# Block 1 of a two-block decoder layer: the first norm's scale moves from the input to the results of the products

## The chip, the cores and the metric

The kernel runs on one core of a Trainium2 chip. A time is the device time of one execution in microseconds (us); a kernel's time is the median over its runs. In the trace PE is the matrix engine, PEld its loading of the stationary operand, DVE the vector engine, ACT the scalar engine, POOL the general-purpose engine and SP the engine whose queue issues most DMA transfers. Times inside a profile count from the start of its span.

## The reference, cut to what matters

A token has 1024 values, there are 256 tokens, and everything is fp32. The first block begins like this:

```python
def rmsnorm(x, g):
    xf = x.astype(jnp.float32)
    y = xf * lax.rsqrt(jnp.mean(xf * xf, axis=-1, keepdims=True) + EPS) * g.astype(jnp.float32)
    return y.astype(x.dtype)

h = rmsnorm(x, attn_pre_norm[l])
proj = h @ w_in[l]
a_cols, f_cols, m_cols = jnp.split(proj, [SWA_COLS, SWA_COLS + FOX_COLS], axis=-1)
```

`a_cols` holds queries, keys and values of a sliding-window attention (512, 128 and 128 columns), `f_cols` queries, keys, values and four gate logits of a forgetting attention (256, 256, 256, 4), `m_cols` the latents of a third attention (416 columns), whose parts get norms of their own. Three attentions, an output product, a convolution feed-forward, and a second block (gated linear attention, pooling, a mixture of 32 experts) follow; none of them is touched. The mean of squares is one number per token, so the norm's scale can be multiplied onto the row of `proj` as well as onto the row of `x`.

## The kernel before, in words

Tokens are two tiles of 128 (t = 0, 1). `x` lies with tokens on partitions; a product needs the contracted dimension there, so `x` is transposed on PE, 128x128 at a time, against an identity matrix loaded from memory (`c_ident`). To keep fp32 accuracy every operand of a large product is split into a high part (a rounded copy, ACT, line 228 for weights and 445 for `hT`) and a low part (the rest, DVE, lines 229 and 446), and a product is three matmuls for each 128 contracted rows: high by high, high by low, low by high (line 131 holds every matmul).

`first_norm(t)` (lines 433 to 447) takes the sum of squares of tile t, forms the reciprocal root (five short DVE steps and one ACT step, line 406), multiplies the scale onto both halves of the tile (`xs`, line 439), transposes eight 128x128 pieces into two PSUM banks, and evacuates each piece twice, as `hH` (ACT, with the norm's gain `g_col` as a column per partition) and as `hL` (DVE). `g_col` comes by a transfer that gathers 1024 single values into columns (line 478).

All weights pass through a ring of four 1 MB buffers `raw`. `add_load` lists the loads in order, `pump(n)` issues the next n, and `drop` hands a buffer back and issues one more. The order here is `vf` (388 columns: both value groups and the gate logits, in two loads by rows, each in two column pieces), `sk` (keys), `sq` 0 and 1 (queries), `ml` 0 and 1 (latents), `fq`, `fk`, then the output product's weights. The x tiles are issued ahead of them on SP.

A unit is a piece of a product: `prep` splits its weights, `run` multiplies and evacuates. `feed` runs a list of units with the `prep` of three further ones ahead. `units_a` (`vf`, `ml`) has tokens on the result's partitions: two PSUM banks, one for each tile; for `vf` the matmuls of tile 1 are held until the last `vf` weights and then run in one go. `unit_b` (`sk`, `sq`, `fq`, `fk`) has columns on partitions and both tiles beside each other, 8 x 3 matmuls of 256 columns. Results are evacuated by `vf_evac` (656, 657), `k_evac` (650, which writes each key group to both partition halves), and `act.mul` or `act.copy` for queries and `fk` (661, 925, 926).

Behind the first query unit stands `bias_rows` (606): a small matmul, a DVE addition (609), a store to memory (`dsc`), two loads that read it back in a skewed form (POOL's queue), and two DVE copies (616) into `bias`, which the sliding-window scores need. The constant `tri` of the gate sums (782) is issued on POOL's queue behind these.

The order of each engine's instructions is set ahead of time by the framework's planner: it walks the program with a model of durations and lets each engine take what is ready in the model, earlier program order first. On the chip an engine then keeps that order, whatever comes late. `issue_after(i)` puts the block's instructions behind instruction i.

Of the kernel before, what the change touches and what calls it, by code (L numbers as in the profile page):

```python
# [9 lines left out]
F32 = mybir.dt.float32  # L10
# [90 lines left out]
def emit(ctx, tc, I, C, out, dump=None, stop=None):  # L101
# [272 lines left out]
    last_pow, last_sq, last_v = [None], [None], [None]  # L374
# [15 lines left out]
    def rstd_halves(h0, h1, dve_half, by_sqrt=False):  # L390
# [14 lines left out]
        if by_sqrt:  # L405
            act.activation(out=r[:, 1:2], in_=v[:, 0:1], func=ACTF.Sqrt)
            dve.reciprocal(r[:, 2:3], r[:, 1:2])
            dve.scalar_tensor_tensor(out=r[:, 3:4], in0=r[:, 2:3], scalar=r[:, 2:3], in1=v[:, 0:1],
                                     op0=ALU.mult, op1=ALU.mult)
            dve.tensor_scalar(out=r[:, 4:5], in0=r[:, 3:4], scalar1=-0.5, scalar2=1.5, op0=ALU.mult, op1=ALU.add)  # L410
            dve.tensor_tensor(out=r[:, 0:1], in0=r[:, 4:5], in1=r[:, 2:3], op=ALU.mult)
            return r
# [20 lines left out]
    def first_norm(t):  # L433

        h0, h1 = x[:, t, 0:512], x[:, t, 512:1024]
        r = rstd_halves(h0, h1, t == 0, True)
        for q in range(2):
            xs = yp.tile([128, 512], F32, name="xs", tag="xs", bufs=2)
            dve.tensor_scalar(out=xs, in0=x[:, t, q * 512:(q + 1) * 512], scalar1=r[:, 0:1], scalar2=None, op0=ALU.mult)
            b = bank()  # L440
            for i in range(4):
                last_mm[0] = pe.transpose(b[:, tk(i)], xs[:, tk(i)], ident)
            for i in range(4):
                k = 4 * q + i
                act.mul(hT[0][:, k, tk(t)], b[:, tk(i)], g_col[:, k:k + 1])
                dve.scalar_tensor_tensor(out=hT[1][:, k, tk(t)], in0=b[:, tk(i)], scalar=g_col[:, k:k + 1],
                                         in1=hT[0][:, k, tk(t)].bitcast(F32), op0=ALU.mult, op1=ALU.subtract)
# [31 lines left out]
    ident = cload("ident", [128, 128], eng=act)  # L479
# [17 lines left out]
    for i in range(2):  # L497
        cols_load(("vf", i), w1, 4 * i, 4, 640, 128, 388, [(128, 1280, 260)])
# [71 lines left out]
    pump(NA)  # L570
# [3 lines left out]
    keep_warm(0, ones)  # L574
    for t in range(2):
        first_norm(t)
        keep_warm(0 if t else 4)
    dump("hH", hT[0].bitcast(F32))
    dump("hL", hT[1].bitcast(F32))
    if stop == "hT":  # L580
        return
# [64 lines left out]

    def k_evac(ps):
# [7 lines left out]
    def vf_evac(t, ps):  # L655
        dve.tensor_tensor(out=fz[:, t, :], in0=ps[:, 384:388], in1=fbB, op=ALU.add)
        act.copy(vf[:, t, :], ps[:, 0:384])
# [3 lines left out]
             + [cols_unit("sq", c // 2, c % 2, lambda ps, c=c: act.mul(qT[:, c, :], ps, 0.125)) for c in range(4)])  # L661
    feed(units[:6] + [then(bias_rows)] + units[6:])
# [252 lines left out]
    def mla_v(kt, h):  # L915
# [5 lines left out]
    feed(units_a("ml", 416, hT, lambda t, ps: ml_ps.__setitem__(t, ps)), rr(swa_all, gate_steps), 2)  # L921
# [3 lines left out]
    feed([cols_unit("fq", 0, c, lambda ps, c=c: act.mul(fqT[:, c, :], ps, 0.125)) for c in range(2)]  # L925
         + [cols_unit("fk", 0, c, lambda ps, c=c: act.copy(fkT[:, c, :], ps)) for c in range(2)], side, 3)
# [911 lines left out]
```

## Time and profile before

| | us |
|---|---|
| median of 3 runs (lowest, highest) | 720.93 (720.68, 722.7) |
| the profiled execution: its own time | 718.01 |
| the profiled execution: its span | 716.2 |
| PE busy in the span | 655.2 (91%) |
| DVE busy | 377.4 (53%) |
| ACT busy | 307.1 (43%) |

The profiled execution is 1.8 us longer than its span, which runs from the first to the last instruction. A busy PE is not a PE at its peak, since matmuls overlap; where PE is dense, one 128x256 matmul starts 0.12 us after the one before it. The chain of waits that ended last lies on PE's matmuls for 59% of the span, and for 20% on the transfers of the expert weights, which fill the stretch from 513 to 653 us.

### The profile page before, as it was taken

How to read it: one execution, taken by the hardware profiler on the slowest of the kernel's cores; microseconds unless marked ns; L12 is line 12 of the kernel's file. 1: busy time of each engine (PE TensorE's matmuls, PEld its weight loads, DVE VectorE, ACT ScalarE, POOL GpSimd, SP SyncE). 2: the span in 40 equal slices, each digit the busy share in tenths (PEclk: the TensorE clock that was granted, in tenths of full speed). 3: DMA queues.
4: the chain of work that ended last, by engine and by line, in shares of the span. 5: the costliest groups of instructions: out<-in, count | busy, mean ns of one | idle time of the engine just before them, and what ended most of it. 6: DMA issues, size and time to landing. Idle time of an engine off the chain costs nothing.

```text
span 716.2 us, 12560 instructions
## 1 busy us (share of the span) xinstructions
PE 655.2 (91%) x5084; PEld 536.4 (75%) x5084; DVE 377.4 (53%) x735; ACT 307.1 (43%) x580; POOL 43.1 (6%) x76
## 2 busy tenths in 40 slices
PE   5999899999999999999999999998999897786992
PEld 4988787999999999978988999987454543442650
DVE  6666577797778777673552755948232211120112
ACT  6739545475657555552932455535220101020111
POOL 5010020100000000002140000000000000000000
PEclk9999999999999999999999999999999999898996
DMA  9973309536556855661392499668999999999971
GB/s 279 322 240 124 112 1 343 174 132 240 197 184 193 278 177 177 220 192 34 89 240 59 153 357 391 232 228 317 381 416 422 423 422 423 423 421 424 422 257 63
DMA packets 82560, 182.31 MB, mean 255 GB/s; under 512 B 10689, under 2 KB 58049, under 8 KB 72256
## 3 DMA queue, kind: packets, MB, share of 16 engines
q1 hardware_dynamic: 78544, 175.27, 67.3%
q0 software_dynamic: 2624, 5.84, 2.6%
q8 instruction: 42, 0.69, 0.4%
q10 hardware_dynamic: 1328, 0.33, 0.2%
q14 instruction: 22, 0.18, 0.1%
HBM read 180.40 MB, written 1.06 MB: 253 GB/s over the span
## 4 chain that ended last, share of the span: by engine, by line
PE 62%; DMA 23%; DVE 6%; issue 4%; ACT 3%; POOL 1%; POOLq 0%; DVEq 0%; SPq 0%; ACTq 0%
PE bank L131 59%; DMA raw<-in_w_exp_up_dram 7%; DMA raw<-in_w_exp_gate_dram 7%; DMA raw<-in_w_exp_down_dram 6%; DMA S<-in_const_tri_dram 1%; DVE wL L229 1%; DMA S<-in_const_oh_rel_dram 1%; ACT S L681 1%; PE bank L689 1%; DMA dsc<-S 1%; DMA S<-in_pool_scale_dram 1%; DVE S L730 1%; PE bank L430 0%; DVE x L458 0%; DVE bank L454 0%
## 5 line engine op out<-in xcount | busy, mean ns | idle before, releaser
L229 DVE TENSOR_TENSOR wL<-raw,wH 128x1024 fp32r<-128x1024 f32 (+3 forms) x120 | 140.6, 1175 | 70.9 <-ACT wH L228 70.5
L228 ACT ACTIVATE wH<-raw 128x1024 fp32r<-128x1024 f32 (+3 forms) x120 | 121.7, 1022 | 109.7 <-PE bank L131 95.0
L131 PE MATMUL bank<-hH,wH 128*128 128x256 f32 (+1 forms) x496 | 141.8, 286 | 0.2 <-ACT wH L228 0.2
L131 PE MATMUL bank<-hL,wH 128*128 128x256 f32 (+1 forms) x496 | 140.2, 283 | 0.0
L131 PE MATMUL bank<-hH,wL 128*128 128x256 f32 (+1 forms) x496 | 140.1, 283 | 0.0
L131 PEld LDWEIGHTS bank<-hH,wH 128*128 128x128 f32 (+1 forms) x496 | 94.3, 190 | 3.2 <-ACT wH L228 1.2
L131 PEld LDWEIGHTS bank<-hL,wH 128*128 128x128 f32 (+1 forms) x496 | 94.3, 190 | 0.8
L131 PEld LDWEIGHTS bank<-hH,wL 128*128 128x128 f32 (+1 forms) x496 | 94.3, 190 | 0.3
L131 PE MATMUL bank<-raw,xg 128*32 128x256 f32 x1024 | 75.8, 413 | 13.9 <-DMA raw<-in_w_exp_up_dram 12.1
L131 PEld LDWEIGHTS bank<-raw,xg 128*32 128x32 f32 x1024 | 36.9, 118 | 45.0 <-DMA raw<-in_w_exp_up_dram 15.6
L1711 ACT ACTIVATE a<-bank,wsl 128x256 f32<-128x256 f32 x8 | 3.8, 474 | 108.8 <-PE bank L131 108.8
L1458 DVE SCALAR_TENSOR_TENSOR a<-bank,wsl,a 128x256 f32<-128x256 f32 x8 | 3.9, 483 | 82.2 <-ACT a L1711 82.2
L986 DVE SCALAR_TENSOR_TENSOR u<-bank,convp,u 128x255 f32<-128x255 f32 (+1 forms) x88 | 41.6, 479 | 6.9 <-ACT u L983 5.7
L131 PE MATMUL bank<-wH,hH 128*128 128x512 f32 (+3 forms) x108 | 39.9, 370 | 0.3 <-ACT hH L237 0.3
L131 PE MATMUL bank<-wH,hL 128*128 128x512 f32 (+3 forms) x108 | 39.1, 362 | 0.2 <-DVE hL L238 0.2
L131 PE MATMUL bank<-wL,hH 128*128 128x512 f32 (+3 forms) x108 | 38.7, 360 | 0.6 <-DVE wL L229 0.6
L131 PE MATMUL bank<-hH,wHL 128*128 128x256 f32 x192 | 36.6, 283 | 0.0
L1747 ACT ACTIVATE y<-bank,wsl 128x256 fp32r<-128x256 f32 (+1 forms) x24 | 13.1, 545 | 52.3 <-PE bank L131 52.2
L1458 DVE SCALAR_TENSOR_TENSOR y<-bank,wsl,y 128x256 fp32r<-128x256 f32 (+1 forms) x24 | 13.2, 570 | 39.4 <-ACT y L1747 39.3
L131 PEld LDWEIGHTS bank<-hH,wHL 128*128 128x128 f32 x192 | 30.8, 192 | 0.2
L983 ACT ACTIVATE u<-bank,convp 128x256 f32<-128x256 f32 x44 | 24.1, 554 | 12.9 <-PE bank L131 10.4
L229 DVE TENSOR_TENSOR wHL<-raw,wHL 128x1024 fp32r<-128x1024 f32 (+2 forms) x23 | 27.5, 1201 | 3.8 <-ACT wHL L228 3.8
(387 smaller groups left out, 1178.5 us busy)
## 6 DMA issues: line engine op xcount, KB each, us to landing
raw<-in_w_exp_gate_dram SPq DMA_DIRECT2D x28, 1024.0 KB, 19.7
raw<-in_w_exp_up_dram SPq DMA_DIRECT2D x28, 1024.0 KB, 19.8
raw<-in_w_exp_down_dram SPq DMA_DIRECT2D x24, 1024.0 KB, 19.7
raw<-in_w_up_dram SPq DMA_DIRECT2D x22, 1024.0 KB, 6.3
raw<-in_w_in_dram SPq DMA_DIRECT2D x20, 1024.0 KB, 5.9
raw<-in_w_down_dram SPq DMA_DIRECT2D x11, 1024.0 KB, 6.8
raw<-in_w_out_dram SPq DMA_DIRECT2D x8, 1024.0 KB, 5.7
raw<-in_w_exp_down_dram SPq DMA_DIRECT2D x12, 512.0 KB, 8.7
```

The lines of the kernel that those rows point to most:

```text
L131: last_mm[0] = pe.matmul(o, lhsT=l, rhs=r, start=start, stop=stop_, **kw)
L228: act.activation(out=hv, in_=raw, func=ACTF.Copy)
L229: dve.tensor_tensor(out=lv, in0=raw, in1=hv.bitcast(F32), op=ALU.subtract)
L681: act.activation(out=S[:, i, :nk], in_=S[:, i, :nk], func=ACTF.Exp, bias=nm[:, i:i + 1], accum_out=l[:, i:i + 1])
L689: pe.transpose(b[:, tk(i)], P[:, i, tk(kt)], ident)
L730: dve.tensor_tensor_reduce(out=Ss[h // 4][:, h % 4, 0:nk], in0=bv[par][:, i, :], in1=bias[:, h, 256 - nk:256], op0=ALU.add, op1=ALU.max, s ...
L983: act.activation(out=u[:, i, :], in_=ps, func=ACTF.Identity, scale=convp[:, 2, jj:jj + 1], bias=convp[:, 3, jj:jj + 1])
L986: dve.scalar_tensor_tensor(out=u[:, i, d:], in0=ps[:, 0:256 - d], scalar=convp[:, 2 - d, jj:jj + 1], in1=u[:, i, d:], op0=ALU.mult, op1=AL ...
L1458: return dve.scalar_tensor_tensor(out=o, in0=a, scalar=sc, in1=b, op0=op0, op1=op1)
L1711: act.activation(out=a, in_=gu[:, 0:256], func=ACTF.Silu, scale=rsl)
L1747: act.mul(y[:, 0, 0:n], db, wsl)
```

## The change

Four things change, all in block 1.

The first loads: x tile 0, then the first `vf` load (now in four pieces, two rows of blocks at a time), then x tile 1, then the other weights. The identity goes first on ACT's queue; the gain comes as eight rows of 128 values and is turned into columns by one transpose on PE and a DVE copy.

`x_in(t)` transposes x unscaled, straight from the loaded tile, and evacuates it with the gain as before. Only then come the squares and the root of tile t, which end in `r1[:, t]`. `x_in(0)` stands ahead of the products, `x_in(1)` behind the second `vf` unit.

The scale goes on the results. Where tokens lie on partitions it is a column: `vf_evac` multiplies by `r1[:, t]` in the same two instructions, and `ml_evac` adds one ACT instruction that scales the bank in place. Where tokens lie along the free dimension, `scale_rows` builds a tile with the scales of all 256 tokens in every partition (a DVE multiplication of the identity, a matmul with ones, a DVE copy), and keys, queries, `fq` and `fk` are evacuated by DVE with `scaled`.

Six small matmuls on the identity (`keep_warm`) stand behind `x_in(0)`; before, there were four, behind tile 0.

```diff
+    def raw_to_hT(t, gain, hT, q):
+        b = bank()
+        for i in range(4):
+            last_mm[0] = pe.transpose(b[:, tk(i)], x[:, t, 512 * q + 128 * i:512 * q + 128 * i + 128], ident)
+        for i in range(4):
+            k = 4 * q + i
+            last_hH[0] = act.mul(hT[0][:, k, tk(t)], b[:, tk(i)], gain(k))
+            last_low[0] = dve.scalar_tensor_tensor(out=hT[1][:, k, tk(t)], in0=b[:, tk(i)], scalar=gain(k),
+                                                   in1=hT[0][:, k, tk(t)].bitcast(F32), op0=ALU.mult,
+                                                   op1=ALU.subtract)
+
+    def scale_rows(o, r, dg):
+        diag_rows(dg, r, 2)
+        b = bank()
+        mm(b[:, 0:256], ones, dg.rearrange("p t s -> p (t s)"), True, True)
+        dve.tensor_copy(out=o, in_=b[:, 0:256])
...
     dma(x[:, 0, :], I["x"][0, tk(0), :])
-    dma(x[:, 1, :], I["x"][0, tk(1), :])
-    g_col = const.tile([128, 8], F32, name="g_col")
-    dma(g_col, I["attn_pre_norm"].rearrange("o (k p) -> p (o k)", p=128), act)
     ident = cload("ident", [128, 128], eng=act)
+    g_row = yp.tile([128, 512], F32, name="xs", tag="xs", bufs=2)[0:8, 0:128]
+    dma(g_row, I["attn_pre_norm"].rearrange("o (k p) -> (o k) p", p=128), act)
+    g_col = const.tile([128, 8], F32, name="g_col")
+    r1 = const.tile([128, 2], F32, name="r1")
...
-    pump(NA)
+    pump(1)
+    dma(x[:, 1, :], I["x"][0, tk(1), :])
+    pump(NA - 1)
...
-    for t in range(2):
-        first_norm(t)
-        keep_warm(0 if t else 4)
+    b = bank()
+    pe.transpose(b[:, 0:8], g_row, ident[0:8, 0:8])
+    dve.tensor_copy(out=g_col, in_=b[:, 0:8])
+
+    def x_in(t):
+        for q in range(2):
+            raw_to_hT(t, lambda k: g_col[:, k:k + 1], hT, q)
+        with tc.issue_after(last_hH[0].ins), tc.issue_after(last_low[0].ins):
+            rstd_halves(x[:, t, 0:512], x[:, t, 512:1024], True, True, out=r1[:, t:t + 1])
+
+    x_in(0)
+    keep_warm(6)
...
+    def second_x():
+        with tc.issue_after(last_mm[0].ins):
+            x_in(1)
...
+    def scaled(o, ps, c_=1.0, p=slice(0, 128)):
+        dve.scalar_tensor_tensor(out=o, in0=ps, scalar=c_, in1=rB1[0][p], op0=ALU.mult, op1=ALU.mult)
+
     def k_evac(ps):
+        scale_rows(rB1[0], r1, rB1[1])
         for g in range(2):
             for r in range(2):
-                (act.copy if r else dve.tensor_copy)(kT[64 * r:64 * r + 64, g, :], ps[64 * g:64 * g + 64, :])
+                p = slice(64 * g, 64 * g + 64)
+                scaled(kT[64 * r:64 * r + 64, g, :], ps[p, :], p=p)
...
-             + [cols_unit("sq", c // 2, c % 2, lambda ps, c=c: act.mul(qT[:, c, :], ps, 0.125)) for c in range(4)])
-    feed(units[:6] + [then(bias_rows)] + units[6:])
+             + [cols_unit("sq", c // 2, c % 2, lambda ps, c=c: scaled(qT[:, c, :], ps, 0.125)) for c in range(4)])
+    feed(units[:2] + [then(second_x)] + units[2:6] + [then(bias_rows)] + units[6:])
...
+    def ml_evac(t, ps):
+        act.mul(ps, ps, r1[:, t:t + 1])
+        ml_ps[t] = ps
...
-    feed([cols_unit("fq", 0, c, lambda ps, c=c: act.mul(fqT[:, c, :], ps, 0.125)) for c in range(2)]
-         + [cols_unit("fk", 0, c, lambda ps, c=c: act.copy(fkT[:, c, :], ps)) for c in range(2)], side, 3)
+    feed([cols_unit("fq", 0, c, lambda ps, c=c: scaled(fqT[:, c, :], ps, 0.125)) for c in range(2)]
+         + [cols_unit("fk", 0, c, lambda ps, c=c: scaled(fkT[:, c, :], ps)) for c in range(2)], side, 3)
```

## Rows read from the trace of the kernel before

**Rows 1.** Waits of PE, 0 to 60 us: who for whom, us in total, times, longest.

```profile
PE bank L442 <- DVE xs L439: 7.6, 1, 7.6
PE bank L131 <- ACT trr L794: 0.6, 1, 0.6
```

**Rows 2.** Stretches: length, then busy us of PE, PEld, DVE, ACT, POOL; clock, DMA share, GB/s.

```profile
10.00:15.00 5.00, 4.42 (x28) 3.98 (x28) 4.61 (x13) 4.82 (x13) 2.28 (x5) 1.00 1.15 325
15.00:20.00 5.00, 4.76 (x26) 4.14 (x25) 4.62 (x12) 3.22 (x8) 0.00 (x0) 1.00 1.05 366
70.00:75.00 5.00, 5.00 (x33) 3.53 (x31) 4.96 (x14) 1.09 (x3) 0.00 (x0) 1.00 0.84 271
```

**Rows 3.** Timeline of PE: start, us, engine, line, operation, names, shape, count.

```profile
11.69 0.42 PE L131 MATMUL bank<-wH,hH 128*128 128x388 f32 x1
...
22.14 0.28 PE L131 MATMUL bank<-hH,wL 128*128 128x256 f32 x1
...
24.77 0.28 PE L131 MATMUL bank<-hH,wH 128*128 128x256 f32 x1
...
27.74 0.81 PE L131 MATMUL bank<-S 32*8 32x384 f32 x2
...
40.05 1.13 PE L131 MATMUL bank<-kT,qT 64*128 64x256 f32 x8
...
43.59 1.16 PE L131 MATMUL bank<-kT,qT 64*128 64x128 f32 x16
```

**Rows 4.** Timeline of ACT; in brackets the idle time before and what ended it.

```profile
1.24 0.60 ACTq L134 DMA_DIRECT2D c_ident<-in_const_ident_dram  x1
...
4.58 0.63 ACT L395 ACTIVATE junk<-x 128x512 bf16<-128x512 f32 x1 [1.43 <-DMA x<-in_x_dram]
...
7.11 0.63 ACT L395 ACTIVATE junk<-x 128x512 bf16<-128x512 f32 x1 [1.27 <-DMA x<-in_x_dram]
...
10.19 0.85 ACT L228 ACTIVATE wH<-raw 128x776 fp32r<-128x776 f32 x1 [0.86 <-DMA raw<-in_w_in_dram]
...
20.64 2.01 ACT L228 ACTIVATE wH<-raw 128x1024 fp32r<-128x1024 f32 x2 [2.00 <-DMA raw<-in_w_in_dram]
```

**Rows 5.** DMA issues: queue, operation, count, KB each, us from issue to landing.

```profile
c_ident<-in_const_ident_dram ACTq DMA_DIRECT2D x1, 64.0 KB, 6.2
...
g_col<-in_attn_pre_norm_dram ACTq DMA_DIRECT2D x1, 4.0 KB, 5.0
```

**Rows 6.** Groups of instructions, 0 to 50 us: busy us, mean ns, idle before.

```profile
L446 DVE SCALAR_TENSOR_TENSOR hL<-bank,g_col,hH 128x128 fp32r<-128x128 f32 x16 | 4.8, 342 | 0.7 <-ACT hH L445 0.7
...
L439 DVE TENSOR_SCALAR xs<-x,rsr 128x512 f32<-128x512 f32 x4 | 1.8, 484 | 0.1
...
L661 ACT ACTIVATE qT<-bank 128x256 f32<-128x256 f32 x4 | 1.5, 375 | 0.7 <-PE bank L131 0.7
...
L397 DVE CUSTOM_DVE_ANT_0 yg<-x 128x512 f32<-128x512 f32 x1 | 0.7, 692 | 3.5 <-DMA x<-in_x_dram 3.5
```

**Rows 7.** Timeline of DVE, 21 to 45 us.

```profile
21.73 1.23 DVE L229 TENSOR_TENSOR wL<-raw,wH 128x1024 fp32r<-128x1024 f32 x1 [1.23 <-ACT wH L228]
...
25.88 0.41 DVE L650 COPY kT<-bank 64x256 f32<-64x256 f32 x1
...
28.20 1.23 DVE L229 TENSOR_TENSOR wL<-raw,wH 128x1024 fp32r<-128x1024 f32 x1 [0.66 <-ACT wH L228]
29.46 0.55 DVE L609 TENSOR_TENSOR S<-bank,S 8x384 f32<-8x384 f32 x1
...
41.18 0.69 DVE L616 COPY bias<-S 128x1024 f32<-128x1024 f32 x1 [7.18 <-DMA S<-dsc]
...
43.96 0.69 DVE L616 COPY bias<-S 128x1024 f32<-128x1024 f32 x1 [1.15 <-DMA S<-dsc]
```

**Rows 8.** The chain that ended last, 30 to 46 us: start, us, what.

```profile
30.30 5.04 DMA dsc<-S
...
37.16 7.53 DMA S<-in_const_tri_dram
```

More of the change, by code (lines that the diff above doesn't have):

```diff
@@ L388, in diag_rows, with rstd_halves @@
                           in1=r[:, 0:n, None].to_broadcast([128, n, 128]), op=ALU.mult)
-    def rstd_halves(h0, h1, dve_half, by_sqrt=False):
+    def rstd_halves(h0, h1, dve_half, by_sqrt=False, out=None):
         s = sm.tile([128, 2], F32, name="ssq", tag="ssq")
@@ L410, in rstd_halves @@
             dve.tensor_scalar(out=r[:, 4:5], in0=r[:, 3:4], scalar1=-0.5, scalar2=1.5, op0=ALU.mult, op1=ALU.add)
-            dve.tensor_tensor(out=r[:, 0:1], in0=r[:, 4:5], in1=r[:, 2:3], op=ALU.mult)
+            dve.tensor_tensor(out=r[:, 0:1] if out is None else out, in0=r[:, 4:5], in1=r[:, 2:3], op=ALU.mult)
             return r
@@ L431, in norm_to_hT @@
             split_act([h[:, 4 * q:4 * q + 4, tk(t)] for h in hT], v3(b, 4, 128))
[L433 to L447, printed above, removed]
+    def raw_to_hT(t, gain, hT, q):
[13 more added lines that the diff above has]
+        dve.tensor_copy(out=o, in_=b[:, 0:256])
     def post(y, t, g):
@@ L497, in emit @@
     for i in range(2):
-        cols_load(("vf", i), w1, 4 * i, 4, 640, 128, 388, [(128, 1280, 260)])
+        add_load(("vf", i), [(lambda t, k=k, d0=d0, nn=nn: v3(t, 4, 388)[:, k:k + 2, d0:d0 + nn],
+                              w1[:, 4 * i + k:4 * i + k + 2, cc:cc + nn])
+                             for k in (0, 2) for d0, cc, nn in ((0, 640, 128), (128, 1280, 260))])
     cols_load(("sk", 0), w1, 0, 8, 512, 128)
@@ L645, in emit @@
     vf, fz = at("vf", [128, 2, 384]), at("fz", [128, 2, 4])
+    rB1 = []
+    def second_x():
+        with tc.issue_after(last_mm[0].ins):
+            x_in(1)
+        yg = yp.tile([128, 1024], F32, name="yg", tag="yg")
+        rB1.append(yg[:, 0:256])
+        rB1.append(v3(yg, 2, 128, 256))
+    def scaled(o, ps, c_=1.0, p=slice(0, 128)):
+        dve.scalar_tensor_tensor(out=o, in0=ps, scalar=c_, in1=rB1[0][p], op0=ALU.mult, op1=ALU.mult)
     def k_evac(ps):
+        scale_rows(rB1[0], r1, rB1[1])
         for g in range(2):
             for r in range(2):
-                (act.copy if r else dve.tensor_copy)(kT[64 * r:64 * r + 64, g, :], ps[64 * g:64 * g + 64, :])
+                p = slice(64 * g, 64 * g + 64)
+                scaled(kT[64 * r:64 * r + 64, g, :], ps[p, :], p=p)
     def cols_unit(key, i, c, evac):
@@ L655, in vf_evac @@
     def vf_evac(t, ps):
-        dve.tensor_tensor(out=fz[:, t, :], in0=ps[:, 384:388], in1=fbB, op=ALU.add)
-        act.copy(vf[:, t, :], ps[:, 0:384])
+        r = r1[:, t:t + 1]
+        dve.scalar_tensor_tensor(out=fz[:, t, :], in0=ps[:, 384:388], scalar=r, in1=fbB, op0=ALU.mult, op1=ALU.add)
+        act.mul(vf[:, t, :], ps[:, 0:384], r)
     units = (units_a("vf", 388, hT, vf_evac, True)
              + [unit_b(("sk", 0), lambda r: v3(r, 8, 128), 8, 128, hT, k_evac, True)]
-             + [cols_unit("sq", c // 2, c % 2, lambda ps, c=c: act.mul(qT[:, c, :], ps, 0.125)) for c in range(4)])
-    feed(units[:6] + [then(bias_rows)] + units[6:])
+             + [cols_unit("sq", c // 2, c % 2, lambda ps, c=c: scaled(qT[:, c, :], ps, 0.125)) for c in range(4)])
+    feed(units[:2] + [then(second_x)] + units[2:6] + [then(bias_rows)] + units[6:])
     b = bank()
```

11 lines of the change are left out of this document (3 added, 8 removed).

## The prediction

> **What bounds the kernel now.** I read the waits of PE first. In the first 60 us PE waits once for long, 7.6 us at the start, for the scaled halves of x (`xs`), and once for 0.6 us, for the `tri` constant [rows 1]. So block 1 has one gap worth the name, and behind it stands what feeds PE. The table of stretches comes next: from 10 to 20 us ACT and DVE are busy 8.0 and 9.2 of 10 us, while PE already counts as busy with matmuls that start one by one [rows 2]. In that stretch the reader should see that PE is paced by the splitting of weights and x, and that PE becomes dense only when the held `vf` matmuls of tile 1 are running. The timeline of ACT shows the third supplier: x tile 0 lands at 4.6, tile 1 at 7.1, the first `vf` weights at 10.2, the first query weights (`sq` 0) at 20.6, each time with ACT waiting [rows 4]. The share of the DMA engines is 1.05 to 1.15 there [rows 2], so these landings follow from the bytes ahead in the queue. Last comes the chain: from 30.3 to 44.7 us it runs through the store of the bias rows and the load of `tri` [rows 8], while PE works through queries and latents and ends up 0.6 us too early [rows 1]. From about 28 to 45 us both are equally long, so a gain counts only if the bias addition (line 609) moves as well as PE.
>
> **The start.** Removed ahead of the first transpose are the squares, the root and four `xs` of 0.48 us [rows 6]. The identity lands at 1.24 + 6.2 = 7.4 us [rows 4, 5], behind the gain, whose 4 KB take 5.0 us [rows 5]; without the norm it alone would hold PE until then. It goes first now, with eight rows instead of 1024 values behind it. Its landing is bounded by x tile 0, eight times as large, at 4.6 [rows 4], and by its old 6.2 us from half a microsecond earlier, 6.9; I take 4.6, nearest to a row without the single values. Weights lose x tile 1 in front of them: from tile 1 to `vf` 0 took 10.2 - 7.1 = 3.1 us [rows 4], so `vf` 0 is whole at 4.6 + 3.1 = 7.7 and its first half at about 6.1; with a high part of 0.85 us [rows 4] the first product starts near 7.2 instead of 11.69 [rows 3]. By the late identity the transposes come 2.3 us later, about 1.0 of it spare while the weights land and are split: 8.5. The lead here is 3 to 4.5 us.
>
> **Four loads become eight.** From tile 1 on, two `vf` transfers landed within 3.1 us [rows 4], the same rate as the 2.5 us of tile 1 alone for its smaller size, so I price the division at nothing; the cover is a queue that holds work until 20 us. The Trainium skill, DMA: Bandwidth & Descriptors, section Anatomy of one DMA, gives every transfer a fixed cost of some 2.0 us and its rules ask for 1 MB or more at a time. By that, four more transfers would cost 8 us if they stood one behind the other; two transfers in 3.1 us say that they overlap.
>
> **To the end of `vf` and `sk`.** DVE loses the four `xs` (1.8 us), gains one sum of squares (0.69 us [rows 6]), and does the eight low parts of tile 0 (8 x 0.34 = 2.7 us [rows 6]) before the weights land, where it used to be idle. The last `vf` matmul ended at about 22.1 [rows 3]. It cannot come earlier than the first product's lead allows (17.6), nor, if only DVE's 1.1 us and half of the 2.7 count, later than 19.7; I take 18.3. The 24 `sk` matmuls at 0.12 us follow (2 were done ahead, the other 22 last from 22.14 to 24.77 [rows 3]): 21.2.
>
> **The first query unit is where the lead shrinks.** Its weights landed at 20.6 with all the bytes ahead of them unchanged [rows 4]. Only the single values of the gain are gone; x tile 0 lands maybe 0.5 us earlier for it, so 20.1 to 20.6. High part 1.0 [rows 4], low part 1.23 [rows 7]: before, the low part was done at 22.96, with PE at the third matmul of the unit, which needs it, at 24.77 + 0.24 = 25.0 [rows 3, 7]. There are 2.05 us of slack, 2.55 with the earlier landing. So of about 4 us, 2.05 to 2.6 remain; I take 2.6, since 1024 separate values are the one thing in that queue unlike all others.
>
> **The bias addition.** Its matmul starts at 27.74 [rows 3], now 25.1. On DVE come new ahead of it: two more key evacuations at 0.41 [rows 7], a scale tile of 256 columns and its copy (bounded by 0.34 for 128 columns [rows 6] and 0.69 for 1024 [rows 7]; 0.4 each), one query evacuation (0.41, which took ACT 0.375 [rows 6]): together 2.0 us. DVE was idle for 1.23 and 0.66 us there, waiting for ACT's high parts [rows 7], which covers 1.9. So the addition moves from 29.46 [rows 7] to about 26.9; without that cover, to 28.5. The matmul with ones costs PE between 0.28 (a split 128x256) and 0.8 us (two of 384 columns) [rows 3]; none of it stays, as PE would otherwise wait from 21.2 for the query weights. The transfers behind the addition take 14.4 us as before [rows 8].
>
> **Later parts.** The two in-place scalings of `ml` cost ACT 0.4 to 0.6 us each by its 256-column row of 0.375 [rows 6]; I take nothing for them, because the latents wait for DVE's scores, and 0.5 as the bound. `fq` and `fk` add four evacuations to DVE, two of them near 66 to 75 us, where DVE is busy 4.96 of 5 us [rows 2]: 0 to 0.8, I take 0.3, since the other two fall where DVE has room. From there on every queue, buffer and transfer is released by computation, so the lead is handed on whole.
>
> **Sum.** 2.6 - 0 - 0.3 = 2.3 us. The profiled execution took 718.01 for a span of 716.2; it would take 715.7. The median of the runs is 2.9 above that execution, so I put the same 2.3 us on the median: 720.93 - 2.3 = 718.6. The forecast's own range is a gain of 1.6 to 3.0, or 717.9 to 719.3.
>
> **Rivals.**
> DVE eats the lead. The four key evacuations (4 x 0.41 = 1.7 us) become ready at 21 us, just when the first query's low part does; if they stand ahead of it, the unit starts 1.7 later and 0.9 remains: 720.0. For it: DVE takes ready work in program order, and the key unit precedes. Against: the query's weights are prepared three units ahead, so they precede in the program.
>
> The query weights land earlier. The gain rows of the output norm (line 670) are issued behind the last root, which now comes later; they and their successor are 128 copies of 4 KB each, 1 MB in all, and at 366 GB/s [rows 2] take 3 us of the same DMA engines. If they fall behind the query weights, the lead of `sk` is kept: 24.77 - 21.2 = 3.6, to 4.3 with `vf` at its early bound, less 0.3 for DVE: about 4, or 716.9. Against: nothing but that hint holds POOL back.
>
> Slower: query evacuations caught behind the bias copies. Queries leave PSUM on DVE now, and DVE stands still for 7.18 us until the read-back lands at 41.2, and again until 44.0 [rows 7]. PE needs queries 0 and 1 at 40.05 [rows 3]. If the planner, which models the transfers as faster, sets both copies ahead of query 1, that evacuation ends at 43.96 + 0.69 + 0.41 = 45.1, PE stands 5 us, 0.6 of which the wait for `tri` gives back: 4.4 lost against 2.6 gained, 722.7. It decides from query 1: if only queries 2 and 3 are caught, the scores at 43.59 [rows 3] wait until 45.5, 1.3 us net of the 0.6, and it is still faster. Against: query 1's product, the next after the bias matmul, is finished by 28.5 + 2.9 = 31.4, 10 us before the copies could run.
>
> Transfers don't overlap. Should each of the four extra ones hold the queue 0.9 us, a third of the pair's 3.1 us [rows 4], the query weights land 3.6 us later, at 23.7; the unit starts 1 us late instead of 2.6 early: 721.9. The skill's fixed cost per transfer, named above, would speak for it, and the trace against it.
>
> **How the numbers follow.** Forecast 0.47, DVE eats the lead 0.25, earlier weights 0.15, caught queries 0.11, serial transfers 0.02. A difference under 0.3%, 2.2 us, is what a measurement of this kernel can't tell from none, and the forecast lies just beyond it: I count 0.38 of its 0.47 as faster and 0.09 as same. Faster is 0.38 + 0.15 = 0.53, same 0.09 + 0.24 + 0.02 = 0.35, slower 0.11 + 0.01 = 0.12. The range reaches from 716.4, past the earlier weights, to 721.9 and leaves out the caught queries.
>
> **What would show it.** Right, if the first transpose starts near 4.6 and the first product near 7.2, PE is dense from about 14, ACT's wait for the first query weights grows and PE waits for their low part at about 22, and the bias addition and the landing of `tri` are both 2 to 3 us earlier. A first product later than 9, an addition later than 28.5, or a PE wait for `qT` near 38 to 45 us would show the step that is wrong. A lead that is there at 45 us and gone at the end would make the whole forecast wrong.

## The result, and the profile after

| | before | after |
|---|---|---|
| median, us (lowest to highest) | 720.55 (717.09 to 722.7), 20 runs | 726.75 (721.95 to 731.44), 20 runs |
| the profiled execution: own time, span | 718.01, 716.2 | 724.18, 722.4 |
| PE, DVE, ACT busy in it | 655.2, 377.4, 307.1 | 659.1, 381.5, 304.9 |

The ratio is 1.009, 95% interval [1.0073, 1.0107]: the change costs 6.2 us, where 2.3 us of gain had been forecast, and the time lies outside the range. One of the twelve runs of e15 below counts as slow; without it the median there is 723.91 us.

**Where it goes.** ACT loads a new function table at fixed places of the program, which makes milestones. These are the ones at the feed-forward and at the second block's products, and the last one ahead of the experts, before and after:

```profile
143.38 1.28 ACT L990 ACT_TABLE_LOAD   x1
355.38 1.28 ACT L1172 ACT_TABLE_LOAD   x1
495.10 1.28 ACT L141 ACT_TABLE_LOAD   x1
```

```profile
148.82 1.28 ACT L1025 ACT_TABLE_LOAD   x1
361.06 1.28 ACT L1207 ACT_TABLE_LOAD   x1
500.32 1.28 ACT L141 ACT_TABLE_LOAD   x1
```

Of the 6.2 us between the two spans, 5.4 are there at the first milestone. Up to the second 0.2 come in, up to the third 0.5 go, and the rest, 1.0, comes behind it. So there are two places to look: the first block, and a small loss near the end.

**The first block.** The waits of PE from 0 to 60 us, which answer to [rows 1]:

```profile
PE bank L584 <- DMA xs<-in_attn_pre_norm_dram: 5.5, 1, 5.5
PE bank L131 <- DVE yg L387: 3.7, 1, 3.7
PE bank L131 <- DVE wL L229: 0.9, 2, 0.6
PE bank L131 <- ACT wH L228: 0.5, 1, 0.5
PE bank L131 <- DVE hL L442: 0.3, 1, 0.3
```

The start is 2.1 us shorter, and a wait of 3.7 us is new: `yg` (line 387) is the identity multiplied by the scales, the operand of the matmul with ones. PE's timeline, against [rows 3], shows where it stands:

```profile
9.61 0.42 PE L131 MATMUL bank<-wH,hH 128*128 128x388 f32 x1
...
25.12 0.28 PE L131 MATMUL bank<-hH,wL 128*128 128x256 f32 x1
29.14 0.67 PE L131 MATMUL bank<-yg,ones 128*128 128x256 f32 x2 [3.74 <-DVE yg L387]
29.46 0.47 PE L131 MATMUL bank<-hH,wH 128*128 128x256 f32 x1
...
34.11 0.81 PE L131 MATMUL bank<-S 32*8 32x384 f32 x2
...
51.06 2.05 PE L131 MATMUL bank<-trr,lfr 128*128 128x256 f32 x16
```

The first product starts 2.1 us earlier than before, but the last `sk` matmul, at 25.12, starts 0.5 us later than the 24.65 of before: the lead is gone before the wait begins. Then PE stands behind the matmul with ones. The 24 matmuls of the first query unit take 4.6 us, from 29.46 to 34.1, where they took 2.9 before; the bias matmul is 6.4 us late and `trr` 5.7.

The table of stretches (length, then busy us of PE, PEld, DVE, ACT, POOL; clock, DMA share, GB/s) says why the query unit is slow:

```profile
10.00:15.00 5.00, 4.28 (x25) 3.29 (x24) 4.65 (x13) 4.06 (x11) 2.29 (x5) 1.00 1.14 335
15.00:20.00 5.00, 3.94 (x22) 3.35 (x21) 3.76 (x13) 3.10 (x7) 0.00 (x0) 1.00 1.05 367
27.00:30.00 3.00, 0.85 (x5) 0.83 (x6) 2.00 (x8) 1.28 (x3) 0.00 (x0) 0.98 1.05 342
30.00:34.00 4.00, 4.00 (x23) 3.98 (x21) 1.97 (x5) 2.38 (x4) 0.00 (x0) 0.59 0.79 252
```

After PE's idling the granted clock falls to the lower of its two levels: from 29.9 to 33.3 us it is 0.50, which is 1.2 GHz, and matmuls start 0.21 us apart instead of 0.12. It falls once more behind PE's wait of 2.2 us for `pt`, the transposed probabilities of an attention, which ends at 87.42. This time it lasts 6.8 us (87.9 to 94.7), where the kernel before has 3.4 us of it (85.8 to 89.2):

```profile
88.00:94.00 6.00, 6.00 (x30) 6.00 (x30) 0.69 (x1) 2.24 (x8) 0.00 (x0) 0.50 0.00 0
```

PE is busy throughout, so the longer half clock makes 1.7 of the 5.4 us.

The chain of waits shows what PE waited for (start, us, what):

```profile
19.84 5.46 PE bank L131 x35
25.34 0.04 issue
25.39 1.06 ACT wH L228
26.47 1.23 DVE wL L229
27.70 0.08 DVE rsr L407
...
28.67 0.34 DVE yg L387
29.01 0.14 issue
29.14 14.59 PE bank L131 x100
```

The root of tile 1 is not slow, it is queued. Its square root is one ACT instruction of 0.19 us, but it stands at 26.35, in ACT's order behind two weight splits. The second of them writes into a buffer that PE's `sk` matmuls hold until 25.34, so it can't start before 25.39. DVE's steps of the root stand behind the low part of the same weights:

```profile
25.39 1.06 ACT L228 ACTIVATE wH<-raw 128x1024 fp32r<-128x1024 f32 x1 [0.25 <-PE bank L131]
26.35 0.19 ACT L406 ACTIVATE rsr<-rsv 128x1 f32<-128x1 f32 x1
```

```profile
26.47 1.23 DVE L229 TENSOR_TENSOR wL<-raw,wH 128x1024 fp32r<-128x1024 f32 x1
27.61 0.16 DVE L407 RECIPROCAL rsr<-rsr 128x1 f32<-128x1 f32 x1
```

So PE waits for a scale that waits for a split that waits for PE. In this order, an earlier `sk` should end in the same stall; no run tries it.

### The profile page after: what moved, and what is told of

The parts are those of the page before. It is cut to its first block, busy times and chain, and to the rows that moved or that the text cites. A ratio compares the mean times of both kernels' runs of the same rounds, so it can differ in the third digit from the quotient of the medians.

```text
span 722.4 us, 12579 instructions
## 1 busy us (share of the span) xinstructions
PE 659.1 (91%) x5091; PEld 540.1 (75%) x5091; DVE 381.5 (53%) x746; ACT 304.9 (42%) x570; POOL 43.1 (6%) x76
## 4 chain that ended last, share of the span: by engine, by line
PE 67%; DMA 18%; DVE 6%; ACT 5%; issue 2%; POOL 0%; SPq 0%; ACTq 0%; POOLq 0%; DVEq 0%
PE bank L131 64%; DMA raw<-in_w_exp_down_dram 6%; DMA raw<-in_w_exp_up_dram 6%; DMA raw<-in_w_exp_gate_dram 5%; ACT S L711 2%; DVE wL L229 1%; ACT wH L228 1%; PE bank L719 1%; DMA xs<-in_attn_pre_norm_dram 1%; PE bank L430 0%; ACT junk L395 0%; DVE x L462 0%; DVE bank L458 0%; DVE xs L426 0%; ACT hH L237 0%
## 5 line engine op out<-in xcount | busy, mean ns | idle before, releaser
L131 PE MATMUL bank<-raw,xg 128*32 128x256 f32 x1024 | 73.9, 399 | 15.1 <-DMA raw<-in_w_exp_up_dram 12.8
L131 PEld LDWEIGHTS bank<-raw,xg 128*32 128x32 f32 x1024 | 35.4, 114 | 45.9 <-DMA raw<-in_w_exp_up_dram 17.2
```

The source lines that it names most:

```text
L131: last_mm[0] = pe.matmul(o, lhsT=l, rhs=r, start=start, stop=stop_, **kw)
```

## The experiments

Times are medians; each ratio, with its 95% interval, is to the kernel before, run on the same chip beside it (medians there 719.68 to 720.53), and isn't the quotient of the two medians. The variants e1 to e3 and e5 to e8 change one thing in the changed kernel or build on one another as said.

**e1: the scale tile from constants.** The keys and queries (and `fq`, `fk`) are multiplied by 1 instead of by their scales; all instructions stay.

```diff
+    rc = const.tile([128, 2], F32, name="rc")
+    dve.memset(rc, 1.0)
-        scale_rows(rB1[0], r1, rB1[1])
+        scale_rows(rB1[0], rc, rB1[1])
```

> The scale tile of the keys and queries is built from a constant, so keys and queries stay unscaled: the matmul with ones no longer waits for the root of tile 1; everything else is the changed kernel. Theory (the wait): PE's stall of 3.7 us ahead of that matmul goes, and with it the half clock of 3.4 us that follows it; the bias matmul moves from 34.1 to about 28.7 and the median falls by about 5 us, to 721 to 722. Rival (DVE): the loss comes from the evacuations that moved to DVE, which are all still there; the time stays near 726. Rival (loads): the loss comes from x tile 1 arriving behind the first weights; the time stays near 726.

720.61 us, ratio 0.9993 [0.9959, 1.0027].

```profile
25.39 0.67 PE L131 MATMUL bank<-yg,ones 128*128 128x256 f32 x2 [0.24 <-DVE yg L387]
28.86 0.81 PE L131 MATMUL bank<-S 32*8 32x384 f32 x2
```

The dependence on the root takes the stall and the half clock away, and 5.2 us at the bias matmul. The whole 6.1 us of time may not be put down to that, because `rc` also moved the buffers behind it (e13 to e16).

**e2: tile 1's squares and root ahead of its transposes.** The result is complete.

```diff
     def x_in(t):
+        if t:
+            rstd_halves(x[:, t, 0:512], x[:, t, 512:1024], True, True, out=r1[:, t:t + 1])
         for q in range(2):
             raw_to_hT(t, lambda k: g_col[:, k:k + 1], hT, q)
+        if t:
+            return
```

> The whole result is computed. Squares and root of tile 1 come ahead of its transposes in the program, without being put behind its evacuations. Theory (the wait): the root is ready near 18 instead of 28.4, the matmul with ones finds its input, the bias matmul is at about 29 and the median falls to about 721 to 722, as with the constant. Rival (DVE): no gain, 726. Rival (loads): no gain, 726, since x lands as before.

723.14 us, ratio 1.0036 [1.0008, 1.0063]. The matmul with ones comes at 19.27 without a wait, the bias matmul at 28.52. Order alone takes 5.6 us away at that place; against the kernel before 0.8 us are left there. At the first milestone (145.45) it is 3.4 us ahead of the changed kernel and 2.1 behind the kernel before; 1.7 of these 2.1 are the half clock behind the wait for `pt`, 6.8 us here as in the changed kernel.

**e3: scale tile and key evacuations behind the first query unit**, which is evacuated by `q0_evac`.

```diff
-    def k_evac(ps):
+    def q0_evac(ps):
+        k_late(k_ps[0])
+        scaled(qT[:, 0, :], ps, 0.125)
+    def k_late(ps):
         scale_rows(rB1[0], r1, rB1[1])
...
-    unit_b(("sk", 0), lambda r: v3(r, 8, 128), 8, 128, hT, k_evac, True)
+    unit_b(("sk", 0), lambda r: v3(r, 8, 128), 8, 128, hT, k_ps.append, True)
```

> The scale tile and the key evacuations come behind the matmuls of the first query unit; the root of tile 1 stays where the changed kernel has it. Theory (the wait): PE uses 2.9 us of the 3.7 for the query unit and waits some 0.7 us behind it; no half clock, the bias matmul at about 30 to 31, the median near 723. Rival (DVE): the same work on DVE, 726. Rival (loads): 726.

726.1 us, ratio 1.007 [1.0046, 1.0094]. PE's wait for `yg` shrinks to 0.8 us, at 28.93, the bias matmul comes at 29.56, and the feed-forward's milestone at 146.02, 2.8 us ahead of the changed kernel's. The median doesn't show it. In its profile the granted clock falls to 0.5 at 383, 397 and 499 us, where the changed kernel's shows nothing. Inconclusive by time, for the stall by trace.

**e4: the kernel before with the new loads alone** (identity first, gain as rows and `vf` in four pieces as in the change; the norm as before).

```diff
-    dma(x[:, 1, :], I["x"][0, tk(1), :])
...
-    pump(NA)
+    pump(1)
+    dma(x[:, 1, :], I["x"][0, tk(1), :])
+    pump(NA - 1)
```

> The kernel before with nothing but the new loads: identity first, the gain as eight rows with one transpose, the first weights in four pieces ahead of x tile 1. Theory (the wait): no wait for a scale is added, so the time is that of before within 1.5 us (719 to 722); x tile 1 lands 2 us later but tile 0 is free 2 us earlier. Rival (loads): the late tile 1 costs, 724 to 726. Rival (DVE): as before, 720.5.

725.73 us, ratio 1.0074 [1.0052, 1.0097]; PE's largest wait:

```profile
PE bank L442 <- DVE xs L439: 7.5, 2, 4.8
```

The first product starts only at 18.36, behind tile 1's transposes in PE's order, whose norm waits for the later x. The load order is worth having only with the raw transposes.

**e5: PE kept busy in the stall.**

```diff
+        keep_warm(16)
         scale_rows(rB1[0], r1, rB1[1])
```

> The changed kernel with 16 small matmuls on the identity in PE's queue ahead of the matmul with ones, so that PE works while it waits for the scale tile. Theory (3.7 us of wait, and 1.7 us of half clock as its consequence): the wait for the tile's arrival stays, ones matmul at 29.1 as in the changed kernel, but no stretch at granted clock 0.5 near 30, first query unit 2.9 us instead of 4.6, bias matmul at 32.4 instead of 34.1, time about 725. Rival (the half clock near 30 has nothing to do with PE's idling): it stays at 30, bias matmul 34.1 or later, time 726.7 or more.

724.02 us, ratio 1.0064 [1.0047, 1.0081]. The stretches of this run:

```profile
27.00:30.00 3.00, 2.92 (x24) 2.68 (x23) 2.07 (x8) 1.39 (x3) 0.00 (x0) 1.00 1.04 338
30.00:34.00 4.00, 4.00 (x30) 3.22 (x30) 2.94 (x8) 3.17 (x5) 0.00 (x0) 1.00 0.75 240
```

The matmul with ones stays at 28.94, the clock stays at 1.00, the bias matmul comes at 32.44 instead of 34.11. The half clock follows the idling and costs 1.7 us; the time fell by 2.7. The Trainium skill (TensorE: Matmul & The Clock Gate, section What's actually happening) says that an idle PE falls to 1.2 GHz. The trace agrees here, but not after every wait: behind the 2.2 us for `pt`, at 85.76, this execution shows no half clock, and e11, e15 and e17 below show none either.

**e6, e7: tile 1 first.** e6 is e2 with tile 1's transposes and evacuations planned with priority; e7 also runs the bias rows ahead of the first query unit.

```diff
+        with tc.high_priority() if t else ExitStack():
             for q in range(2):
                 raw_to_hT(t, lambda k: g_col[:, k:k + 1], hT, q)
...
-    feed(units[:2] + [then(second_x)] + units[2:6] + [then(bias_rows)] + units[6:])
+    feed(units[:2] + [then(second_x)] + units[2:5] + [then(bias_rows)] + units[5:])   # e7
```

> Tile 1's squares and root first (as in the run with the root first), and its transposes and high parts planned with priority, ahead of the high part of the first query weights. Theory (the lead of the first product, 2.1 us, was lost because tile 1's last high part stood behind the query weights' in ACT's order): tile 1's last high part by 18.5 instead of 21.7, last key matmul done by 23 to 23.5, first query unit at 23.1 to 23.5 (the query weights' low part is done at 23.0 and bounds it), bias matmul at 26 to 26.5 against 27.7 before, time 718.5 to 719.5. Rival (the matmuls up to the keys are paced by the weights' splitting whatever the order of tile 1): last key matmul still at 25 to 25.5, time as with the root first alone, 722 to 723.

722.86 us, ratio 1.004 [1.0021, 1.0059]. The rival was right: tile 1's last high part moves from 21.70 to 18.2, and the last `sk` matmul only from 25.12 to 24.42. From the first product at 9.44 to that point PE issues 48 matmuls of 388 columns, 24 of 256 and tile 1's eight transposes, which at their spacing of 0.175, 0.12 and 0.1 us are 12.1 us without a gap; it takes 15.0. The waits between are small and each for another part (0.3 for `hL`, 0.4 for `hH`, 0.3 for `wL` are the ones listed): DVE is busy 13.6 of these 15.0 us and ACT 11.5, so a part that is moved ahead seems to make another late; that is argued and not tried.

> The kernel of the run with priority for tile 1, with the bias rows' matmul and addition also moved ahead of the first query unit. Theory (PE's lead counts only if the bias addition moves with it): bias matmul at 23 to 24, addition done by 25, tri in PE's reach by 41 to 42 instead of 45, no wait of PE for trr; 0 to 1 us less than with the priority alone. Rival (tri is not late with that lead, or DVE's bias copies now stand ahead of something): the same time or up to 1 us more.

721.61 us, ratio 1.0017 [0.9992, 1.0041]. The bias matmul comes at 25.29 and the addition at 27.62, later than the 23 to 24 and 25 expected; `tri` is read at 40.99 and PE doesn't wait for `trr` (45.13), as expected. The first milestone, at 142.97, is at last level with the kernel before, and the time still shows no gain.

**e8: no scaling of keys and queries** (e2 with the evacuations of the kernel before; the scaling of keys, queries, `fq` and `fk` is left out).

```diff
-        scale_rows(rB1[0], r1, rB1[1])
...
-                scaled(kT[64 * r:64 * r + 64, g, :], ps[p, :], p=p)
+                (act.copy if r else dve.tensor_copy)(kT[64 * r:64 * r + 64, g, :], ps[64 * g:64 * g + 64, :])
```

> Tile 1's squares and root first; keys, queries, fq and fk are left unscaled and evacuated by the instructions of the kernel before, and the scale tile with its matmul with ones is gone (part of the computation is left out). Theory (the root's lateness is what cost, the evacuations on DVE are covered): within 1 us of the run with the root first alone, 722 to 723.5, bias matmul near 28.2. Rival (DVE's six more instructions and the ones matmul are on the path): 1.5 us or more below it, 721 or less, bias addition 1.5 us earlier.

723.61 us, ratio 1.0055 [1.0026, 1.0083]; bias addition at 29.46 against 29.96 in e2. The evacuations on DVE are covered, as predicted.

**e9, e10, e12: the other long wait.** In the kernels without the edit below PE waits 2.2 to 2.8 us for `pt`, until some point between 81 and 90 us. These runs put 16 matmuls on the identity there: e9 in e7, e10 in the kernel before, e12 in e5.

```diff
             pts = [transpose_p(Ss[g], kt, (g + kt) % 2) for kt in range(n + 1)]
             yield 1
+            if n and g == 0:
+                with tc.issue_after(last_tr[0].ins):
+                    for _ in range(16):
+                        pe.matmul(ob[:, 0:128], lhsT=ident, rhs=ident, start=True, stop=True)
```

> The kernel with priority for tile 1 and the earlier bias rows, and 16 small matmuls on the identity where PE waits 2.2 us for pt near 79 us (they write the bank that the next matmuls overwrite). Theory (an idle PE is followed by half clock, and all variants of the change pay more of it at 84 us, 6.8 us against 3.4 before): no stretch at granted clock 0.5 between 80 and 95, vf,pt no later than 81.5, ACT's first table load for the feed-forward 3 us earlier than 142.97, time 718.5 to 720, below the kernel before. Rival (the half clock near 84 does not follow from that wait): it is still there, time 721 to 722.

718.78 us, ratio 0.9978 [0.9957, 0.9999].

> The kernel before with the same 16 matmuls in its wait of 2.7 us for pt near 80 us; nothing of the change is in it. Theory: the 3.4 us at half clock at 85.8 go, 1.7 us less, 718.5 to 719.5, so that whatever the run with the earlier bias rows and the same matmuls shows beyond that is the change's. Rival: no difference, 720 to 721, since the clock falls elsewhere instead.

716.57 us, ratio 0.9952 [0.9935, 0.9968]. Stretches before, and in e10:

```profile
79.00:84.00 5.00, 2.29 (x21) 1.89 (x18) 2.62 (x13) 3.11 (x13) 0.00 (x0) 1.00 0.00 0
84.00:94.00 10.00, 10.00 (x79) 10.00 (x78) 5.01 (x10) 4.83 (x15) 0.56 (x1) 0.83 0.00 1
```

```profile
77.00:82.00 5.00, 5.00 (x45) 4.47 (x45) 1.75 (x14) 4.64 (x20) 0.00 (x0) 1.00 0.02 6
82.00:92.00 10.00, 10.00 (x93) 10.00 (x93) 6.24 (x18) 4.64 (x14) 0.56 (x1) 1.00 0.01 2
```

> The changed kernel with 16 small matmuls on the identity in both of PE's long waits, for the scale tile at 25.4 and for pt near 83. Theory (what is left of the loss is the wait of 3.7 us itself): no half clock before 100, the wait's cost alone stays, 722.5 to 724. Rival (the half clock just moves to other places): 726 or more, as the changed kernel.

723.06 us, ratio 1.0031 [1.0008, 1.0053], with no half clock ahead of 495 us. Filling this wait takes 3.7 us off the kernel before, 2.8 off e7 and 1.0 off e5, so it is no merit of the change: e9 is 2.2 us slower than e10, though at the first milestone it is 1.6 us ahead (140.76 against 142.40). Only 1.0 of e10's 3.7 us is there at that milestone (142.40 against 143.38). The rest goes with the granted clock of whole runs, 0.979 on the mean in e10 and 0.972 in the kernel before; why it is higher isn't known.

**e11: e7 with the old order of x and `vf` loads.** The first `vf` load is in two pieces again as well.

```diff
     dma(x[:, 0, :], I["x"][0, tk(0), :])
+    dma(x[:, 1, :], I["x"][0, tk(1), :])
...
-    pump(1)
-    dma(x[:, 1, :], I["x"][0, tk(1), :])
-    pump(NA - 1)
+    pump(NA)
```

> The kernel with priority for tile 1 and the earlier bias rows, but with both x tiles ahead of the weights and the first vf load in two pieces, as in the kernel before (the identity stays first, the gain as rows). Theory (the early first product buys nothing, since PE is paced by the splitting from 10 to 20 us): first product at 11 to 12 instead of 9.4, bias matmul still at 25 to 25.8, time within 1 us of that kernel's 721.6. Rival (the load order is what the lead comes from): bias matmul 1.5 to 2 us later, 723 or more.

723.13 us, ratio 1.0039 [1.0017, 1.0062]. The first product starts at 11.77 after a wait of 2.0 us for `wH`, and the clock is at 0.5 from 12.7 to 19.5 us; the bias matmul comes at 28.67, 3.4 us later than in e7. Up to there the load order does carry the lead; how much of this is the lost clock can't be read from one run. At the first milestone e11 is level with e7 (143.05 against 142.97), because no half clock follows the wait for `pt` in this execution, where e7's has 6.8 us of it.

**e13 to e16: where the buffers lie.** Between 400 and 440 us (for the changed kernel 406 to 446) PE runs the second block's matmuls without a pause, the same ones in both kernels. A group by line (busy us, mean ns), before, after, and in e14 and e16 below:

```profile
L131 PE MATMUL bank<-hL,wH 128*128 128x256 f32 x110 | 30.7, 279 | 0.0
```

```profile
L131 PE MATMUL bank<-hL,wH 128*128 128x256 f32 x107 | 30.3, 283 | 0.0
```

They start 0.117 us apart before, 0.120 after. The new tile `r1` holds 8 bytes in each partition. Taken as rounded up to 32 (no trace shows a buffer's place), it moves the large buffers placed after it by as much, the ring and the split weights among them. e14 is e10 with an unused tile of that size in its place, e13 is e9 with `r1` widened to 64 bytes, e15 the changed kernel so widened, and in e16 (e9 otherwise) `r1` lies in a pool of block 1's attention, so that the second block's buffers lie where they lay before. But for the memset in e14, the order of work on every engine is the same with and without the move.

```diff
-    r1 = const.tile([128, 2], F32, name="r1")
+    r1 = const.tile([128, 16], F32, name="r1")[:, 0:2]   # e13, e15
+    r1 = at("r1", [128, 16])[:, 0:2]                     # e16, e17
+    dummy = const.tile([128, 2], F32, name="dummy")      # e14, with one memset
```

> The kernel with tile 1's priority, earlier bias rows and the matmuls in the wait for pt, with the tile r1 widened from 2 to 16 values (unused ones), so that every buffer behind it lies 64 bytes from its place in the kernel before instead of 32; the order of all engines is the same. Theory (a shift of 32 bytes slows the dense matmuls of the second block): 128x256 matmuls start 0.117 us apart from 400 to 440 us as in the kernel before, instead of 0.120; 1.0 to 1.5 us less between the table loads at 355 and 492 us; time 717 to 718 against 718.8. Rival (the spacing follows from the order of the instructions or from what runs beside them): still 0.120, time 718.8.

716.22 us, ratio 0.9939 [0.9911, 0.9966]. The spacing is 0.118, between the two:

```profile
L131 PE MATMUL bank<-hL,wH 128*128 128x256 f32 x103 | 28.9, 281 | 0.0
```

> The kernel before with the matmuls in its wait for pt, and an unused tile of 2 values (one DVE memset at the start) where the change puts r1, which shifts all buffers behind it by 32 bytes; nothing else of the change. Theory: the spacing from 400 to 440 us goes from 0.117 to 0.120, the stretch between the table loads near 354 and 490 us is 1.0 to 1.5 us longer, time 717.5 to 718.2 against 716.6. Rival: spacing 0.117, time 716.6.

719.65 us, ratio 0.9978 [0.9954, 1.0001]; 3.1 us more than e10, for 32 bytes. Part of this may be the clock, since over whole runs 0.975 was granted here and 0.979 in e10. The spacing is 0.120:

```profile
L131 PE MATMUL bank<-hL,wH 128*128 128x256 f32 x107 | 30.3, 283 | 0.0
```

> The changed kernel with r1 widened from 2 to 16 values, nothing else. Theory: first 143 us as in the changed kernel (stall of 3.7 us, half clock behind it), spacing 0.117 from 400 to 440 us, time 725 to 725.8 against 726.75. Rival: spacing 0.120, 726.8.

724.48 us, ratio 1.0051 [1.0012, 1.0089]: 2.3 to 2.8 us below the changed kernel, with its stall of 3.7 us still there and a spacing of 0.118. The first 143 us are not as expected: this execution has no half clock behind the wait for `pt`, and reaches the first milestone at 145.63, 3.2 us early.

> As the run with the wide r1 in the best variant, but r1 lies in a pool of the first block's attention, so that every buffer of the second block has exactly its place of the kernel before; the order of all engines is again the same. Theory (the place of the buffers alone sets the spacing): 0.117 us between 128x256 matmuls from 400 to 440 us, 135.8 us between the table loads near 353 and 489 us as in the kernel before with the matmuls in the wait for pt (135.80), about 141 at the first feed-forward table load, time 715.2 to 716.2. Rival (half of the wider spacing belongs to the order of the instructions): 0.1185 and 136.4 us as with the wide r1, time 716.2 or more.

715.16 us, ratio 0.9935 [0.9911, 0.996]. The spacing is 0.117 again, and 135.90 us lie between the table loads at 354.34 and 490.24, as in e10 (135.80).

```profile
L131 PE MATMUL bank<-hL,wH 128*128 128x256 f32 x105 | 29.3, 279 | 0.0
```

The second effect lies in the experts' stage, where the DMA engines are fully taken. 150 us of it, from 25 us behind the third milestone on, before, after, in e14 and in e13:

```profile
520.10:670.10 150.00, 123.91 (x1233) 66.86 (x1226) 29.83 (x78) 19.53 (x48) 0.00 (x0) 0.95 1.01 422
```

```profile
525.32:675.32 150.00, 122.89 (x1226) 66.08 (x1215) 29.20 (x77) 19.01 (x47) 0.00 (x0) 0.97 1.01 421
```

```profile
520.55:670.55 150.00, 123.63 (x1245) 66.49 (x1236) 28.94 (x75) 19.03 (x47) 0.00 (x0) 0.97 1.01 421
```

```profile
516.44:666.44 150.00, 125.23 (x1207) 67.92 (x1207) 29.91 (x78) 19.53 (x48) 0.00 (x0) 0.93 1.01 425
```

The weights come at 422 GB/s with buffers in their old places, 421 when moved by 32 bytes, 425 when moved by 64. From the third milestone to the end the profiled executions take 220.2 to 221.3 us in the kernel before, e1, e4, e10, e13, e15 and e17, 222.2 in e16, and 221.8 to 226.6 in all eleven with the 32 bytes. The rate alone would make 0.4 us of that in 150, so it doesn't explain the longer ones.

That the place is the cause of the spacing and the rate is shown, since e14 and e16 change nothing else, and all nineteen profiles sort by it: 0.117 us and 422 GB/s in the old places (the kernel before, e4, e10, e16, e17), 0.120 and 421 in the eleven with the 32 bytes, 0.118 and 425 with 64. Among the last is e1, which has two such tiles ahead of the buffers, as twice 32 would have it. The medians bear the place out as well: e9, e13 and e16 were granted like clocks over their whole runs (0.976, 0.975, 0.977), and e13 is 2.6 and e16 3.6 us below e9. Why 32 bytes matter isn't shown.

**e17: e16 without the matmuls in the wait for `pt`.**

> The same without the matmuls in the wait for pt: what the change is worth by itself once the root comes first, tile 1 has priority, the bias rows go earlier and the buffers of the second block keep their places. Theory: the half clock near 84 us is back, 2 to 3 us above the run with r1 elsewhere, 718 to 719, or 1.5 us below the kernel before. Rival (the lead at 143 us is given back): 720 or more.

718.33 us, ratio 0.9975 [0.9951, 1.0]. This is the idea of the change with the root first, tile 1 preferred, the bias rows earlier and the buffers in their places: 1.3 us better than before in these medians, at the edge of what can be told. e16, which fills the wait as well, beats both kernels by far more than it can be uncertain; it is 1.4 us below e10, by separate comparisons with the kernel before whose intervals overlap.

## Why the prediction was wrong

**The step that failed** is the one on the bias addition: "The matmul with ones costs PE between 0.28 [...] and 0.8 us [...]; none of it stays, as PE would otherwise wait from 21.2 for the query weights." Only the matmul's own length was priced. It stands in PE's queue ahead of the first query unit, and its operand ends a chain of eleven small instructions on ACT and DVE, which take their turns among weight splits of 1.0 to 1.2 us. The wait added is 3.7 us, and its sequel in the clock 1.7 (e5): the addition came at 34.95, where 26.9 had been forecast and 29.46 stood before. The prediction named what is queued behind added DVE work, and never asked when the root of tile 1 comes, which it had itself described as moved behind the transposes.

**The start.** Predicted 4.6 for the first transpose and 7.2 for the first product; measured 5.45 and 9.61, by its own test ("later than 9") wrong. The identity, issued at 0.74, takes 4.4 us where it took 6.2 [rows 5], and so lands half a microsecond later than assumed; the gain's rows land at 5.32, and their transpose stands ahead of x's. The first high part of the weights, at 7.89, is in ACT's order behind two high parts of x that wait for PE's transposes. It is done at 8.73, and the first product starts only at 9.61, because PE's queue holds the twelve small matmuls of `keep_warm(6)` ahead of it and runs them from 7.38 on without a pause:

```profile
5.62 1.97 PE L438 MATMUL bank<-c_ident,x 128*128 128x128 f32 x8
7.38 2.47 PE L131 MATMUL bank<-c_ident 128*128 128x128 f32 x12
```

The prediction gave them no time, and looked at none of these orders. What fewer of them would gain isn't tested.

**To the end of `vf` and `sk`.** Predicted 18.3 and 21.2, measured about 23.8 and 25.2. The estimate took the low parts of tile 0 off the busy stretch, but only two of the eight were done when the first low part of weights began (8.77). And the squares and root of tile 0, done before 10 us in the kernel before, went into it: DVE's lie between 12.35 and 16.04. PE is busy 8.2 of the 10 us from 10 to 20, against 9.2 before [rows 2]. A bound from PE's own work was to be had: 7.2 + 12.1 (e6) is 19.3, so 21.2 left 1.9 us for all gaps, where the best order tried has 2.9 (e6) and the change 3.4 (from 9.61 to 25.12).

**What was right.** The query weights landed at 20.2, as forecast. Their low part didn't gain by it: it was done at 23.05, where it had been at 22.96, because ACT's high part waited for a buffer that PE held until 20.73. PE came too late for it to matter.

```profile
20.73 1.06 ACT L228 ACTIVATE wH<-raw 128x1024 fp32r<-128x1024 f32 x1 [1.69 <-PE bank L131]
```

The four further `vf` transfers cost nothing that shows: the query weights landed no later, and the four pieces of the first `vf` load landed at 5.5, 6.3, 7.1 and 7.7 us. The Trainium skill (DMA: Bandwidth & Descriptors, section Anatomy of one DMA) gives a fixed cost of some 2 us for a transfer that POOL issues. By an estimate from it, four more, one behind the other, would cost 8 us; these are issued by SP, and the trace decides for overlap.

The evacuations on DVE are covered (e8). The fourth query evacuation is caught behind the second bias copy, at 44.88, and does no harm. The 14.4 us taken for the transfers behind the bias addition were too much: ACT reads `tri` at 45.46, 10.0 us after the addition's end, with the DMA engines taken to 0.64 from 36 to 45 us; before, it was 1.08 from 36 to 44. PE, 5.7 us late itself, doesn't wait for it.

**"The lead is handed on whole"** is nearly right for order and queues. It is wrong for two things that aren't in any queue: the places of the buffers (e13 to e16), and the clock, which falls after waits and at other places from run to run. e9, which has both against it, leads e10 by 1.6 us at the first milestone and ends 2.2 behind.

**Slips in its working that decided nothing.** Without the cover the addition comes to 28.9 (26.9 and 2.0), not 28.5; a third of 3.1 us is 1.0, not 0.9; the two `vf` transfers moved 776 KB in 3.1 us, 250 KB per us, and tile 1 came at 205, which isn't the same rate; and beside the wait for `tri` PE had another of 0.6 us, for a low part of weights near 12.9.

What the 6.2 us are made of: filling the stall took 2.7 us off (e5), taking it out by order 3.6 (e2), and giving the buffers other places 2.3 (e15). The differences between these medians are uncertain by 1 to 2 us each, so they aren't added up. At the first milestone, in the profiled executions, order takes 3.4 of the 5.4 us (e2), and 1.7 are the longer half clock behind the wait for `pt`. The clock has a part in the medians as well: over whole runs it is 0.968 on the mean in the changed kernel and 0.971 to 0.973 in the kernel before, and the changed kernel took 721.95 us at 0.976 and 731.44 at 0.961. Open is why the granted clock falls at some places of the second block in one execution and not in another, and with it part of e3.

## What to carry to other kernels

Moving a scale from input to output moves the point by which it must be known, and a matmul that spreads it stands in PE's queue like any other: follow its operand back through every engine's order, above all where that order holds work that waits for PE. Look for long waits of a PE that was busy (2.0 to 3.7 us here), since their sequel in the clock can cost as much as they do; filling one with small matmuls gained 0.5% here without the change, most of it in places far behind it. And compare the spacing of the same matmuls far from the edit: a small new tile placed ahead of the large buffers can slow everything after it.

## What the runs showed of the hardware that was not expected

32 bytes more ahead of the buffers of each partition change the spacing of dense 128x256 matmuls from 0.117 to 0.120 us and the rate of the weight stream from 422 to 421 GB/s; 64 bytes give 0.118 us and 425 GB/s. In all, the kernels with the 32 bytes are 2.3 to 3.6 us of 720 slower than like ones with none or 64 (e10 to e14, e9 to e13 and e16, e15 to the changed kernel), by medians from different chips. The half clock after an idle PE isn't certain: after the wait of 2.2 to 2.8 us for `pt` it came in nine profiled executions, among them e7's, and not in those of e5, e11, e15 and e17.
